# Up projection of a squared-ReLU MLP: one 512-column matmul against both parts of the activations, in place of two of 256

## The chip, the cores and the metric

The kernel runs on one core of one Trainium2 chip. The metric is device time in microseconds, the median of several runs. The engines are named as the profile names them: PE is TensorE's matmul, PEld its weight load, DVE is VectorE, ACT is ScalarE, POOL is GpSimd, SP is SyncE, which here issues nearly all transfers.

## The reference

One decoder layer on 256 positions of 2048 features, all in fp32: RMSNorm, an input projection to two groups of eight heads (forgetting attention, dilated attention), group norms, an output projection, then the MLP with squared ReLU, and a final norm. The change concerns the first product of the MLP:

```
h = rms_norm(x, norm2_g[l])
x = x + jnp.square(jax.nn.relu(h @ w_mlp_in[l])) @ w_mlp_out[l]
return rms_norm(x, final_norm_g)
```

`w_mlp_in` is 2048 x 8192, `w_mlp_out` 8192 x 2048.

## The kernel before

**Precision by parts.** Each fp32 operand is split in two parts of the type float32r: `hi`, a rounded copy, and `lo`, the remainder. A product of two operands is the sum of three matmuls into the same PSUM columns: hi x hi, hi x lo and lo x hi. Activations stand in SBUF by feature: `aT_hi` and `aT_lo` hold 16 tiles (kt) of 128 features x 256 positions each, `hT_hi` and `hT_lo` (which are the buffers `big_hi` and `big_lo`) the same for the hidden layer.

**Chunks and steps.** All weights are streamed once, in chunks of 512 columns: 12 chunks for q, v and k, 8 for the output projection, then four rounds of 4 chunks "u" (up) and 4 chunks "d" (down). A round covers 2048 of the 8192 hidden features. An up or down chunk has 16 kt, two to a step, so 8 steps. For a step the weights of two kt arrive in `raw` (four buffers, two steps each, DMA issued by SP), ACT rounds them into `whi` (line 178) and DVE takes the remainder into `wlo` (line 179); both pools hold four steps.

**Two ways of multiplying.** For "q", "k" and "u" (`TURNED`) the weights are the stationary operand, in blocks of 128 columns, and the activations stream, 256 columns at a time (`turned_product`, line 340): per kt 4 blocks x 3 matmuls. Two blocks share a PSUM bank of 512 columns. The result is already by feature. For "o", "v" and "d" the activations are stationary and 512 weight columns stream (`product`, lines 323 to 325): per kt 2 halves of the positions x 3 matmuls.

**The drain of an up chunk** (`drain_u`) takes each of the two banks through relu (ACT, 626), a square (DVE, 627), the rounded part (ACT, 261) and the remainder (DVE, 262) into `hT_hi` and `hT_lo`.

**What sets the order.** The order is written out by hand; each engine runs its own instructions in that order. Ahead of step i's matmuls stands the split of step i + 3 (`LEAD`), and small work is hung behind single kt by `at(...)`: the drain of a chunk behind its last kt. So on ACT and DVE the drain stands behind the split for three steps ahead and before the split for the step after that. The last chunk of all has a loop of its own (`last_chunk`), and the weights of its first four steps are split into the place of `aT_hi` and `aT_lo`, which nobody needs any more. The PSUM pool has four banks named "acc", two named "sc" and two named "tr", eight in all; "sc" and "tr" serve the attention and the transposes before the MLP.

Of the kernel before, what the change touches and what calls it, by code (L numbers as in the profile page):

```python
# [11 lines left out]
F32 = mybir.dt.float32  # L12
F32R = mybir.dt.float32r
BF16 = mybir.dt.bfloat16
AF = mybir.ActivationFunctionType
ALU = mybir.AluOpType
# [3 lines left out]
P = 128  # L20
D_MODEL = 2048
SEQ = 256
# [5 lines left out]
KT = D_MODEL // P  # L28
CW = 512
# [44 lines left out]
def kernel(  # L74
# [18 lines left out]
    nc = tc.nc  # L93
# [7 lines left out]
    two = ctx.enter_context(tc.tile_pool(name="two", bufs=2))  # L101
    wraw = ctx.enter_context(tc.tile_pool(name="wraw", bufs=4))
    wsplit = ctx.enter_context(tc.tile_pool(name="wsplit", bufs=LEAD + 1))
    wide = ctx.enter_context(tc.tile_pool(name="wide", bufs=1))
    few = ctx.enter_context(tc.tile_pool(name="few", bufs=1))
    psum = ctx.enter_context(tc.tile_pool(name="psum", bufs=2, space=PSUM))
# [4 lines left out]
    chunks = []  # L111
# [25 lines left out]
    raws, splits = {}, {}  # L137
# [15 lines left out]
    def split(i, j0=0, n=2):  # L153
        if i >= len(steps):
            return
        if j0:
            return split_rows(i, j0, n)
        ci, s = steps[i]
        if ci == len(chunks) - 1 and s < 4:
            hi, lo = (a[:, 4 * s:4 * s + 4, :].rearrange("p (k j) s -> p k (j s)", k=2) for a in (aT_hi, aT_lo))  # L160
        else:
            what, cols = chunks[ci][0], chunks[ci][5]
            high, low = (HIGH, LOW) if what in TURNED else (NEAR, NEAR) if cols == CW else (GATED, HIGH - NEAR)
            hi, lo = (
                wsplit.tile([P, 2 * CW + LINE], F32R, name=n)[:, b:b + 2 * cols].rearrange("p (j c) -> p j c", j=2)
                for n, b in (("whi", high), ("wlo", low))
            )
        splits[i] = (hi, lo)
        split_rows(i, j0, n)

    def split_rows(i, j, n):
        ci, s = steps[i]
        hi, lo = (a[:, j:j + n, :] for a in splits[i])
        t = raws[ci, s // 2][:, 2 * (s % 2) + j:2 * (s % 2) + j + n, :chunks[ci][5]]
        cols = t.shape[2]
        step = cols // 2 if i == j == 0 else cols
        for c in range(0, cols, step):
            nc.scalar.activation(hi[:, :, c:c + step], t[:, :, c:c + step], AF.Copy)  # L178
        nc.vector.tensor_tensor(lo, t, hi.bitcast(F32), op=ALU.subtract)  # L179
# [68 lines left out]
        nc.vector.tensor_copy(gT[:, k0:k1], p[:, k0:k1])  # L248

    wide.tile([P, NEAR], F32, name="ahead")  # L250
    aT_hi = wide.tile([P, KT, SEQ], F32R, name="aT_hi")
    aT_lo = wide.tile([P, KT, SEQ], F32R, name="aT_lo")

    def split_psum(hi, lo, src, scale=None, early=False):

        if early:

            nc.vector.tensor_scalar(hi, src, scale, None, op0=ALU.mult)
            nc.vector.scalar_tensor_tensor(lo, src, scale, hi.bitcast(F32), op0=ALU.mult, op1=ALU.subtract)
        elif scale is None:  # L260
            nc.scalar.activation(hi, src, AF.Copy)  # L261
            nc.vector.tensor_tensor(lo, src, hi.bitcast(F32), op=ALU.subtract)  # L262
        else:
            nc.scalar.activation(hi, src, AF.Copy, scale=scale)
            nc.vector.scalar_tensor_tensor(
                lo, src, scale, hi.bitcast(F32), op0=ALU.mult, op1=ALU.subtract
            )
# [42 lines left out]
    accs = {}  # L310

    def operands(what, key):
        if what == "o":
            return yT_hi, yT_lo, key[0] * NH
        if what == "d":
            return hT_hi, hT_lo, 0
        return aT_hi, aT_lo, 0

    def product(acc, a, kt, t, w, j, cols, go, end):

        (ah, al, base), (hi, lo) = a, w
        xh, xl = (p[:, base + kt, t * P:(t + 1) * P] for p in (ah, al))
        nc.tensor.matmul(acc, xh, hi[:, j, cols], start=go, stop=False, skip_group_check=True)  # L323
        nc.tensor.matmul(acc, xl, hi[:, j, cols], start=False, stop=False, skip_group_check=True)  # L324
        nc.tensor.matmul(acc, xh, lo[:, j, cols], start=False, stop=end, skip_group_check=True)  # L325

    def turned_product(ci, i, j, kt, kts):


        if kt == 0:  # L330
            accs[ci] = [psum.tile([P, CW], F32, name="acc", bufs=4) for _ in range(2)]
        hi, lo = splits[i]
        terms = ((hi, aT_hi), (hi, aT_lo), (lo, aT_hi))
        order = [(b, n) for b in range(4) for n in range(3)]
        if i == j == 0:
            order.sort(key=lambda bn: bn[1])
        for b, n in order:
            acc = accs[ci][b // 2][:, b % 2 * SEQ:(b % 2 + 1) * SEQ]
            w, a = terms[n]
            nc.tensor.matmul(acc, w[:, j, b * P:(b + 1) * P], a[:, kt, :],  # L340
                             start=kt == 0 and b % 2 == 0 and n == 0, stop=kt == kts - 1 and n == 2,
                             skip_group_check=True)

    def products(i, j):
        ci, s = steps[i]
        what, key, _, _, _, cols, kts = chunks[ci]
        kt = 2 * s + j
        if what in TURNED:
            return turned_product(ci, i, j, kt, kts)
        a = operands(what, key)  # L350
        if cols > CW:
            return gated_products(ci, i, j, kt, kts, a)
        if kt == 0:
            accs[ci] = [psum.tile([P, CW], F32, name="acc", bufs=4) for _ in range(TB)]
        go, end = kt == 0, kt == kts - 1
        for t in range(TB):
            product(accs[ci][t], a, kt, t, splits[i], j, slice(0, CW), go, end)

    def gated_products(ci, i, j, kt, kts, a):

        if kt == 0:
            accs[ci] = [psum.tile([P, 512], F32, name=n, bufs=k) for n, k in (("acc", 4), ("acc", 4), ("sc", 2))]
        half = CW // 2
        for t in range(TB):
            for acc, c0, c1, go in ((accs[ci][0][:, t * half:(t + 1) * half], 0, half, t == 0),
                                    (accs[ci][1 + t][:, :half + NH], half, CW + NH, True)):
                product(acc, a, kt, t, splits[i], j, slice(c0, c1), go and kt == 0, kt == kts - 1)
# [252 lines left out]
    def drain_u(c, ci):  # L620


        acc = accs.pop(ci)
        for half in range(2):
            h = two.tile([P, CW], F32, name="nat")
            nc.scalar.activation(h, acc[half], AF.Relu)
            nc.vector.tensor_tensor(h, h, h, op=ALU.mult)
            k0 = 4 * c + 2 * half
            split_psum(
                hT_hi[:, k0:k0 + 2, :].rearrange("p k s -> p (k s)"),  # L630
                hT_lo[:, k0:k0 + 2, :].rearrange("p k s -> p (k s)"), h,
            )
# [82 lines left out]
    for ci, (what, key, *_rest) in enumerate(chunks[:-1]):  # L715
# [9 lines left out]
        elif what in "qk":  # L725
            for half in range(2):
                late = half if what == "k" else (2 if key else 8) + 5 * half
                at(e + late, drain_qk, key, what, ci, half)
            if what == "k":
                kind = groups[key][4]  # L730
                for h in range(4):
                    n = e + 6 + 7 * (h // 2)
                    if kind == 0:
                        at(n - 3, decay_of, groups[key][3] * 4 + h)
                    at(n, scores, key, h)
                for h in range(4):
                    at(e + 20 + 7 * (h // 2), values, key, h)
                for h in range(4):
                    at(e + 13 + 7 * (h // 2), turn_probs, key, h)
                if key % 2:  # L740
                    at(e + 33, group_norm, kind)
        elif what == "o":
            at(e, drain_o, *key, ci)
            if key[0] == 1:
                for n in range(2):
                    at(e + 2, to_features, 4 * key[1] + 2 * n, 16)
                if key[1] == 3:
                    at(e + 4, second_norm)
        elif what == "u":
            at(e, drain_u, key[1], ci)  # L750
        else:
            at(e, drain_d, *key, ci)
            if key == (ROUNDS - 1, 0):
                at(e - 8, load_gf)

    idle_products(WARM)
    for k in range(2):
        to_features(k, 0, 1)
        split(0, k, 1)
    idle_products(WARM2)  # L760
    at(0, gains, 2, 16)
    at(0, to_features, 2, 0, 1)
    at(0, split, 1, 0, 1)
    at(0, to_features, 3, 0, 1)
    at(0, split, 1, 1, 1)
# [58 lines left out]
```

## Time and profile before

| | |
|---|---|
| median of 3 runs | 1104.33 us (1104.29 to 1105.59) |
| span of the profiled execution | 1214.1 us |
| its own time beside the span | none is given; the span is the first to the last instruction |
| granted TensorE clock, mean over the span | 0.850 |
| TensorE matmuls | 7373, in progress 1201.8 us |
| TensorE weight loads | 7373, in progress 1070.3 us |
| VectorE, ScalarE | 655.5 and 521.1 us busy |
| DMA | 209.17 MB, mean 172 GB/s |

The page and the views beside it are of one profiled execution, which is longer than the runs. A row of a group gives the source line, the engine, the operation, the tiles written and read, the shapes and the count, then busy time in us and the mean of one in ns, then the engine's idle time before it and who ended it. A row of the timeline gives the start and the length in us. Matmuls overlap, so that the length of one is more than the distance from one to the next; the distances are what counts.

### The profile page before, as it was taken

What the parts mean: (1) busy time and instruction counts of PE and PEld (TensorE: products, weight loads), DVE (VectorE), ACT (ScalarE), POOL (GpSimd) and SP (SyncE); (2) the same over time, 40 slices, a digit from 0 to 9 for tenths busy, and PEclk for the clock granted to TensorE, in tenths of its full rate; (3) what the DMA queues carried; (4) which work ended last, traced back from release to release, by engine and by line L of the source; (5) the groups of instructions that cost most, each with busy time, mean ns of one, the idle gap of its engine ahead of it and who ended that gap; (6) DMA issues with size and microseconds to landing.
All of it is one profiled execution on the core that took longest, in us unless ns stands there. A gap on an engine that the chain in (4) does not pass through costs nothing.

```text
span 1214.1 us, 17573 instructions
## 1 busy us (share of the span) xinstructions
PE 1201.8 (99%) x7373; PEld 1070.3 (88%) x7373; DVE 655.5 (54%) x837; ACT 521.1 (43%) x687; POOL 27.3 (2%) x42
## 2 busy tenths in 40 slices
PE   9999999999999999999999999999999999999997
PEld 8999898998987799987789997779998779998776
DVE  5666656556566655544544455445545444555563
ACT  5454535445444544443334443334444333444341
POOL 0010200000000000000000000000000000000000
PEclk8888888888888888888888888888888888888887
DMA  8664553544544455555555545555655555545541
GB/s 300 200 209 139 169 178 112 190 160 139 184 153 165 148 174 173 161 187 175 176 175 175 173 170 187 179 170 158 194 183 178 174 173 173 174 147 222 187 139 70
DMA packets 105387, 209.17 MB, mean 172 GB/s; under 512 B 3971, under 2 KB 5084, under 8 KB 105180
## 3 DMA queue, kind: packets, MB, share of 16 engines
q1 hardware_dynamic: 104412, 206.59, 51.6%
q8 instruction: 57, 0.93, 0.3%
q0 software_dynamic: 304, 1.06, 0.2%
q10 hardware_dynamic: 592, 0.40, 0.1%
q14 instruction: 22, 0.18, 0.0%
HBM read 205.93 MB, written 2.11 MB: 171 GB/s over the span
## 4 chain that ended last, share of the span: by engine, by line
PE 99%; DMA 0%; DVE 0%; issue 0%; ACT 0%; POOL 0%; ACTq 0%; DVEq 0%
PE acc L340 48%; PE acc L324 16%; PE acc L323 16%; PE acc L325 16%; PE tr L275 1%; PE sc L575 1%; PE sc L531 0%; PE tr L559 0%; DMA xs<-in_x_dram 0%; PE sc L527 0%; PE sc L577 0%; PE sc L323 0%; PE sc L324 0%; PE sc L325 0%; PE sc L521 0%
## 5 line engine op out<-in xcount | busy, mean ns | idle before, releaser
L179 DVE TENSOR_TENSOR wlo<-raw,whi 128x1024 fp32r<-128x1024 f32 (+2 forms) x382 | 464.0, 1223 | 416.9 <-ACT whi L178 414.8
L178 ACT ACTIVATE whi<-raw 128x1024 fp32r<-128x1024 f32 (+2 forms) x383 | 398.7, 1051 | 475.0 <-PE acc L340 230.1
L340 PE MATMUL acc<-aT_hi,whi 128*128 128x256 f32 x1536 | 450.5, 294 | 0.0
L340 PE MATMUL acc<-aT_hi,wlo 128*128 128x256 f32 x1536 | 446.3, 291 | 0.0
L340 PE MATMUL acc<-aT_lo,whi 128*128 128x256 f32 x1536 | 445.7, 291 | 0.0
L340 PEld LDWEIGHTS acc<-aT_hi,whi 128*128 128x128 f32 x1536 | 306.0, 199 | 1.5 <-ACT p L261 0.7
L340 PEld LDWEIGHTS acc<-aT_lo,whi 128*128 128x128 f32 x1536 | 304.8, 199 | 0.4
L340 PEld LDWEIGHTS acc<-aT_hi,wlo 128*128 128x128 f32 x1536 | 304.9, 199 | 0.0
L324 PE MATMUL acc<-whi,big_lo 128*128 128x512 f32 (+1 forms) x632 | 262.4, 415 | 0.0
L323 PE MATMUL acc<-whi,big_hi 128*128 128x512 f32 (+1 forms) x632 | 262.2, 415 | 0.0
L325 PE MATMUL acc<-wlo,big_hi 128*128 128x512 f32 (+1 forms) x632 | 260.6, 412 | 0.0
L323 PEld LDWEIGHTS acc<-whi,big_hi 128*128 128x128 f32 x632 | 121.6, 192 | 36.1
L325 PEld LDWEIGHTS acc<-wlo,big_hi 128*128 128x128 f32 x632 | 121.6, 192 | 35.9
L324 PEld LDWEIGHTS acc<-whi,big_lo 128*128 128x128 f32 x632 | 121.7, 193 | 34.6
L323 PE MATMUL acc<-whi,aT_hi 128*128 128x512 f32 (+1 forms) x144 | 54.7, 380 | 0.0
L324 PE MATMUL acc<-whi,aT_lo 128*128 128x512 f32 (+1 forms) x144 | 54.1, 376 | 0.0
L325 PE MATMUL acc<-wlo,aT_hi 128*128 128x512 f32 (+1 forms) x144 | 54.1, 376 | 0.0
L262 DVE TENSOR_TENSOR big_lo<-nat,big_hi 128x512 fp32r<-128x512 f32 x32 | 22.2, 692 | 22.4 <-ACT big_hi L261 22.4
L650 DVE SCALAR_TENSOR_TENSOR xs<-acc,rstd2sq,xs 128x512 f32<-128x512 f32 (+1 forms) x33 | 24.2, 734 | 16.2 <-PE acc L325 16.2
L325 PEld LDWEIGHTS acc<-wlo,aT_hi 128*128 128x128 f32 x144 | 27.7, 192 | 5.5
L323 PEld LDWEIGHTS acc<-whi,aT_hi 128*128 128x128 f32 x144 | 27.9, 194 | 5.2
L324 PEld LDWEIGHTS acc<-whi,aT_lo 128*128 128x128 f32 x144 | 27.9, 194 | 5.1
(167 smaller groups left out, 508.4 us busy)
## 6 DMA issues: line engine op xcount, KB each, us to landing
raw<-in_w_mlp_in_dram SPq DMA_DIRECT2D x64, 1024.0 KB, 5.3
raw<-in_w_mlp_out_dram SPq DMA_DIRECT2D x64, 1024.0 KB, 5.1
raw<-in_w_in_dram SPq DMA_DIRECT2D x42, 1024.0 KB, 5.0
raw<-in_w_out_dram SPq DMA_DIRECT2D x16, 1024.0 KB, 5.1
raw<-in_w_in_dram SPq DMA_DIRECT2D x4, 1040.0 KB, 8.1
xs<-in_x_dram SPq DMA_DIRECT2D x3, 512.0 KB, 9.8
raw<-in_w_in_dram SPq DMA_DIRECT2D x2, 512.0 KB, 5.7
big_lo<-rel_d POOLq DMA_DIRECT2D x1, 1024.0 KB, 7.0
```

The source lines that it names most:

```text
L178: nc.scalar.activation(hi[:, :, c:c + step], t[:, :, c:c + step], AF.Copy)
L179: nc.vector.tensor_tensor(lo, t, hi.bitcast(F32), op=ALU.subtract)
L262: nc.vector.tensor_tensor(lo, src, hi.bitcast(F32), op=ALU.subtract)
L275: nc.tensor.transpose(p[:, j * SEQ + t * P:j * SEQ + (t + 1) * P], xs[:, t, c:c + P], ident)
L323: nc.tensor.matmul(acc, xh, hi[:, j, cols], start=go, stop=False, skip_group_check=True)
L324: nc.tensor.matmul(acc, xl, hi[:, j, cols], start=False, stop=False, skip_group_check=True)
L325: nc.tensor.matmul(acc, xh, lo[:, j, cols], start=False, stop=end, skip_group_check=True)
L340: nc.tensor.matmul(acc, w[:, j, b * P:(b + 1) * P], a[:, kt, :], start=kt == 0 and b % 2 == 0 and n == 0, stop=kt == kts - 1 and n == 2, s ...
L575: nc.tensor.matmul(y[:, :SEQ], v[:, 0, dims], p[:, m, :SEQ], start=n == 0, stop=False, skip_group_check=True)
L650: nc.vector.scalar_tensor_tensor(xs[:, t, cs], acc[:, :cs.stop - cs.start], rstd2sq[:, t:t + 1], xs[:, t, cs], op0=ALU.mult, op1=ALU.add)
```

## The change

For the up projection alone, `aT_hi` and `aT_lo` become the two halves of one tile `aT`, kt by kt, so that hi and lo of one kt lie side by side as 512 columns. A new function, `paired_product`, gives each block of 128 weight columns a PSUM bank of its own. Per block and kt the hi weights are loaded once, and all 512 columns stream past them: the left half of the bank collects hi x hi, the right half hi x lo. Then the lo weights are loaded and the 256 columns of hi stream into the right half. At the chunk's end the two halves are added, and relu and square become one operation. A chunk takes four banks: two "acc", and two "sc" or two "tr" in turn. "q" and "k" are multiplied as before, with `aT_hi` and `aT_lo` as views.

```diff
         if ci == len(chunks) - 1 and s < 4:
-            hi, lo = (a[:, 4 * s:4 * s + 4, :].rearrange("p (k j) s -> p k (j s)", k=2) for a in (aT_hi, aT_lo))
+            hi, lo = (aT[:, 4 * s + 2 * n:4 * s + 2 * n + 2].rearrange("p k j s -> p k (j s)") for n in range(2))
...
-    aT_hi = wide.tile([P, KT, SEQ], F32R, name="aT_hi")
-    aT_lo = wide.tile([P, KT, SEQ], F32R, name="aT_lo")
+    aT = wide.tile([P, KT, 2, SEQ], F32R, name="aT")
+    aT_hi, aT_lo = aT[:, :, 0], aT[:, :, 1]
...
+    def paired_product(ci, i, j, kt, kts):
+        if kt == 0:
+            rest = ("sc", "tr")[chunks[ci][1][1] % 2]
+            accs[ci] = [psum.tile([P, CW], F32, name=n, bufs=k) for n, k in (("acc", 4), ("acc", 4), (rest, 2), (rest, 2))]
+        hi, lo = splits[i]
+        for b, acc in enumerate(accs[ci]):
+            w = slice(b * P, (b + 1) * P)
+            nc.tensor.matmul(acc.rearrange("p (n s) -> p n s", n=2), hi[:, j, w], aT[:, kt],
+                             start=kt == 0, stop=False, skip_group_check=True)
+            nc.tensor.matmul(acc[:, SEQ:], lo[:, j, w], aT[:, kt, 0],
+                             start=False, stop=kt == kts - 1, skip_group_check=True)
...
+        if what == "u":
+            return paired_product(ci, i, j, kt, kts)
         if what in TURNED:
             return turned_product(ci, i, j, kt, kts)
...
         for half in range(2):
             h = two.tile([P, CW], F32, name="nat")
-            nc.scalar.activation(h, acc[half], AF.Relu)
-            nc.vector.tensor_tensor(h, h, h, op=ALU.mult)
+            n = two.tile([P, CW], F32, name="nat")
+            for k in range(2):
+                part, bank = n[:, k * SEQ:(k + 1) * SEQ], acc[2 * half + k]
+                nc.scalar.activation(part, bank[:, SEQ:], AF.Copy)
+                nc.vector.tensor_tensor(part, bank[:, :SEQ], part, op=ALU.add)
+            nc.vector.scalar_tensor_tensor(h, n, 0.0, n, op0=ALU.max, op1=ALU.mult)
             k0 = 4 * c + 2 * half
```

How the instructions stand, at three places. First TensorE at the first kt of the first up chunk, before; a row is a matmul with its weight load, the numbers tell buffers apart, and `acc_4256` and `acc_4257` are the two banks:

```order
L340 MATMUL acc_4256<-aT_hi_127,whi_4194 128x256
L340 MATMUL acc_4256<-aT_lo_128,whi_4194 128x256
L340 MATMUL acc_4256<-aT_hi_127,wlo_4195 128x256
L340 MATMUL acc_4256<-aT_hi_127,whi_4194 128x256
L340 MATMUL acc_4256<-aT_lo_128,whi_4194 128x256
L340 MATMUL acc_4256<-aT_hi_127,wlo_4195 128x256
L340 MATMUL acc_4257<-aT_hi_127,whi_4194 128x256
L340 MATMUL acc_4257<-aT_lo_128,whi_4194 128x256
L340 MATMUL acc_4257<-aT_hi_127,wlo_4195 128x256
```

The same place now, the whole kt, with four banks:

```order
L353 MATMUL acc_4255<-aT_127,whi_4193 128x512
L355 MATMUL acc_4255<-aT_127,wlo_4194 128x256
L353 MATMUL acc_4256<-aT_127,whi_4193 128x512
L355 MATMUL acc_4256<-aT_127,wlo_4194 128x256
L353 MATMUL sc_4257<-aT_127,whi_4193 128x512
L355 MATMUL sc_4257<-aT_127,wlo_4194 128x256
L353 MATMUL sc_4258<-aT_127,whi_4193 128x512
L355 MATMUL sc_4258<-aT_127,wlo_4194 128x256
```

Three rows of 256 to a block have become one of 512 and one of 256. Next VectorE at the end of that chunk, before, from the drain to the next splits:

```order
L627 TENSOR_TENSOR nat_4512<-nat_4512 128x512
L262 TENSOR_TENSOR big_lo_142<-nat_4512,big_hi_141 128x512
L627 TENSOR_TENSOR nat_4517<-nat_4517 128x512
L262 TENSOR_TENSOR big_lo_142<-nat_4517,big_hi_141 128x512
L179 TENSOR_TENSOR wlo_4523<-raw_4342,whi_4522 128x1024
```

And now:

```order
L646 TENSOR_TENSOR nat_4450<-acc_4255,nat_4450 128x256
L646 TENSOR_TENSOR nat_4450<-acc_4256,nat_4450 128x256
L647 SCALAR_TENSOR_TENSOR nat_4449<-nat_4450 128x512
L262 TENSOR_TENSOR big_lo_141<-nat_4449,big_hi_140 128x512
L646 TENSOR_TENSOR nat_4459<-sc_4257,nat_4459 128x256
L646 TENSOR_TENSOR nat_4459<-sc_4258,nat_4459 128x256
L647 SCALAR_TENSOR_TENSOR nat_4458<-nat_4459 128x512
L262 TENSOR_TENSOR big_lo_141<-nat_4458,big_hi_140 128x512
L179 TENSOR_TENSOR wlo_4468<-raw_4327,whi_4467 128x1024
```

Four adds of half a bank have come in ahead of the next split, which stands where it stood. Last ScalarE at the same place, before:

```order
L626 ACTIVATE nat<-acc 128x512
L261 ACTIVATE big_hi<-nat 128x512
L626 ACTIVATE nat<-acc 128x512
L261 ACTIVATE big_hi<-nat 128x512
L178 ACTIVATE whi<-raw 128x1024 x8
```

And now:

```order
L645 ACTIVATE nat<-acc 128x256 x2
L261 ACTIVATE big_hi<-nat 128x512
L645 ACTIVATE nat<-sc 128x256 x2
L261 ACTIVATE big_hi<-nat 128x512
L178 ACTIVATE whi<-raw 128x1024 x8
```

A relu of 512 columns has become two copies of 256; the splits of the next chunk's eight steps follow as before.

## The prediction, made before the changed kernel ran

> **What bounds the kernel now.** I read the page first, then the chain of work that ended last in order of time, then the busy time of two neighbouring stretches.
>
> ```profile
> span 1214.1 us, 17573 instructions
> PE 1201.8 (99%) x7373; PEld 1070.3 (88%) x7373; DVE 655.5 (54%) x837; ACT 521.1 (43%) x687; POOL 27.3 (2%) x42
> PE 99%; DMA 0%; DVE 0%; issue 0%; ACT 0%; POOL 0%; ACTq 0%; DVEq 0%
> ```
>
> The chain is TensorE from end to end: it hardly waits for anyone. The question is what TensorE itself is held by: the columns that stream through the array, or the weight loads, which it starts as often as matmuls (7373 each).
>
> ```profile
> 627.47 96.33 PE acc L340 x768
> 820.13 96.33 PE acc L340 x768
> ```
>
> These rows of the chain are two whole up-projection stages (round 1 and round 2): 4 chunks x 16 kt x 12 matmuls = 768 each, none missing. Between them, from 627.47 + 96.33 = 723.80 to 820.13, lies the down projection of round 1. The two stretches side by side (the count takes in a neighbour's at the edge):
>
> ```profile
> core 0: us, PE busy (x) PEld busy (x) DVE busy (x) ACT busy (x) POOL busy (x), PEclk, DMA share, GB/s
> 627.47:723.80 96.33, 96.33 (x769) 96.33 (x769) 47.85 (x47) 40.72 (x45) 0.00 (x0) 0.85 0.55 176
> 723.80:820.13 96.33, 96.33 (x386) 73.82 (x386) 46.93 (x43) 35.67 (x36) 0.00 (x0) 0.85 0.53 173
> ```
>
> This is the central reading. The up projection does 768 matmuls of 256 columns, the down projection 384 of 512: both 196,608 columns. The first has twice the matmuls and twice the weight loads, and its loads are in progress 96.33 of 96.33 us, against 73.82. Yet both take 96.33 us. A matmul of 256 costs 96.33/768 = 0.1254 us, one of 512 costs 96.33/384 = 0.2509. So time goes by columns, at one granted clock (0.85), and the 384 additional loads and matmuls cost nothing to within the 0.01 us of the rows. A load row that is always busy is no proof that loads bind.
>
> **How this execution stands to the runs.** The median of the three runs is 1104.33 us, 109.8 below the profiled span; nothing on the page tells of time around the span, so I take the span as the execution's own time.
>
> ```profile
> 0.00:8.00 8.00, 5.64 (x16) 1.00 0.70 194
> 8.00:10.00 2.00, 2.00 (x12) 0.96 1.05 387
> 10.00:1200.00 1190.00, 1188.73 (x7307) 0.85 0.52 173
> 1205.46:1214.10 8.64, 0.00 (x0) 0.58 0.32 122
> ```
>
> (TensorE alone: length, busy, granted clock, DMA.) The clock falls from 1.00 to 0.85 around 9 us and stays there; after 1205.46 no matmul runs. If the runs differ from the profile by their clock alone, the 1195.5 us from 10 to 1205.46 take 1104.33 - 18.6 = 1085.7 in them: an estimated mean clock of 0.85 x 1195.5/1085.7 = 0.936. Nothing shows that clock directly, and this is the weak point of the forecast.
>
> **The change part by part.** *Matmuls and loads.* Per block of 128 weights and kt, three matmuls of 256 with three loads become one of 512 and one of 256 with two loads. Sixteen chunks x 16 kt x 4 blocks = 1024 such groups: 1024 loads and 1024 matmuls vanish (of 7373), the columns stay at 1024 x 768. By the stretches above: before 3 x 0.1254 = 0.376 us, after 0.2509 + 0.1254 = 0.376. Worth 0 in this execution. The cover that makes it so is the stream itself: each load lies under the matmul before it.
>
> How close are loads to binding? In the head work, 128-column transposes stand back to back, with half the columns of an up-projection matmul to hide a load (first row: loads; the others: transposes):
>
> ```profile
> 112.00 0.73 PEld L559 LDWEIGHTS tr<-ident,pr 128*128 128x128 f32 x6
> 12.57 0.42 PE L275 MATMUL tr<-ident,xs 128*128 128x128 f32 x2
> 6.17 0.90 PE L275 MATMUL tr<-ident,xs 128*128 128x128 f32 x3 [1.18 <-DMA xs<-in_x_dram]
> 4.57 0.42 PE L275 MATMUL tr<-ident,xs 128*128 128x128 f32 x1
> L559 PEld LDWEIGHTS tr<-ident,pr 128*128 128x128 f32 x48 | 5.6, 144 | 0.0
> L275 PE MATMUL tr<-ident,xs 128*128 128x128 f32 x64 | 11.7, 302 | 1.2 <-DMA xs<-in_x_dram 1.2
> ```
>
> With 0.14 us for a single such load (144 ns), six in 0.73 are (0.73 - 0.14)/5 = 0.118 us apart. A load thus paces at some 0.118 us where 0.1254 is to be covered: hidden, but by 6% only. After the change two loads (0.236) stand under 0.376.
>
> The Trainium skill, "TensorE: Matmul & The Clock Gate", section "LDWEIGHTS (loading the stationary operand)", puts a load at columns / 1.2 ns, an estimate of 106.7 ns for 128; the trace's 118 decides here. By the page's figure loads would stay hidden at a clock of 0.936 too, where a matmul of 256 takes 0.1254 x 0.85/0.936 = 0.114 us, and the sum would be the same 0.
>
> *The layout* (aT in one tile, kt by kt) changes addresses, no instruction: 0. The rows that split a weight for the last chunk into aT's place are the same in number.
>
> *The drain* of a chunk grows, on ACT and DVE. Round 1's first chunk ends at 627.47 + 24.08 = 651.55:
>
> ```profile
> 650.83 0.60 ACT L626 ACTIVATE nat<-acc 128x512 f32<-128x512 f32 x1 [1.32 <-PE acc L340]
> 652.19 0.63 ACT L261 ACTIVATE big_hi<-nat 128x512 fp32r<-128x512 f32 x1 [0.76 <-DVE nat L627]
> 652.73 0.58 ACT L626 ACTIVATE nat<-acc 128x512 f32<-128x512 f32 x1
> 654.18 0.63 ACT L261 ACTIVATE big_hi<-nat 128x512 fp32r<-128x512 f32 x1 [0.88 <-DVE nat L627]
> 654.72 2.00 ACT L178 ACTIVATE whi<-raw 128x1024 fp32r<-128x1024 f32 x2
> 651.46 0.69 DVE L627 TENSOR_TENSOR nat<-nat 128x512 f32<-128x512 f32 x1 [0.69 <-ACT nat L626]
> 652.85 0.69 DVE L262 TENSOR_TENSOR big_lo<-nat,big_hi 128x512 fp32r<-128x512 f32 x1 [0.70 <-ACT big_hi L261]
> 655.79 2.36 DVE L179 TENSOR_TENSOR wlo<-raw,whi 128x1024 fp32r<-128x1024 f32 x2 [0.26 <-ACT whi L178]
> ```
>
> Queued behind the drain on both engines is the split of the weights of step i+4 (i the chunk's last step). It starts at 654.72 and its wlo is done at 655.79 + 1.23 = 657.02. TensorE wants it three steps after the chunk's end: 651.55 + 3 x 24 x 0.1254 = 660.58. The slack is 3.56 us.
>
> The new operations by their nearest rows: the copy of half a bank like L584, the add like L663 (from SBUF) or the 256-column L650 (from PSUM), the max-and-multiply like L627 above (0.69).
>
> ```profile
> L584 ACT ACTIVATE sqt<-sc 128x256 f32<-128x256 f32 x14 | 5.4, 384 | 5.6 <-DVE sc L583 5.6
> L650 DVE SCALAR_TENSOR_TENSOR xs<-acc,rstd2sq,xs 128x256 f32<-128x256 f32 x2 | 1.0, 484 | 5.5 <-PE acc L325 5.5
> L663 DVE TENSOR_TENSOR xs<-xs,relT 128x256 f32<-128x256 f32 x2 | 0.8, 420 | 0.6 <-ACT nat L657 0.6
> L650 DVE SCALAR_TENSOR_TENSOR xs<-acc,rstd2sq,xs 128x512 f32<-128x512 f32 x31 | 23.2, 750 | 10.7 <-PE acc L325 10.6
> ```
>
> I take 0.38 for a copy and 0.45 for an add, between the two rows. Per chunk ACT goes from 2 x 0.60 + 2 x 0.63 = 2.46 to 4 x 0.38 + 1.26 = 2.8, DVE from 4 x 0.69 = 2.8 to 4 x 0.45 + 2.8 = 4.6: 4 chunks add 7 us to DVE's 47.85 of 96.33. In time: the first copy can begin one block earlier (650.45), the second at 650.83; add to 651.7, max-and-multiply to 652.4, big_hi to 653.0, big_lo to 653.7 with both copies of the second half beside it; two adds to 654.5, max-and-multiply to 655.2, big_hi to 655.8. The split then starts near 655.7 instead of 654.72, 1.0 us late, and the slack is still 2.6. At the runs' 0.936 three steps are 8.2 us and it is 1.8. Worth 0; what hides it is LEAD = 3.
>
> Who else waits for the drain: the down projection wants the last chunk's hT only at kt 12, three quarters into its first chunk (18 us). The four banks of a chunk (two of "acc", two of "sc" or "tr") are written again two chunks, 48 us, later. DMA queues: SP issues the same transfers in the same order; a raw buffer is freed up to 1 us later, with four in turn of 6 us each.
>
> **Sum:** 1214.1 + 0 + 0 = 1214.1 profiled, 1104.3 for the runs.
>
> **The rivals.** *1. Loads bind in the runs, though not in the profile.* If a load keeps its 0.118 us while a matmul of 256 shrinks with the clock, the runs' q, k and u matmuls (4608) are paced by loads. Then 4608 x 0.118 = 544 of the 1085.7 us, the other 1195.5 - 4608 x 0.1254 = 617.7 take 542, the clock is 0.85 x 617.7/542 = 0.969, and the change takes the up projection from 3072 x 0.118 = 362.5 to 1024 x 0.376 x 0.85/0.969 = 337.8: 25 less, 1080. For: the 6% margin. Against: loads follow the clock, since transposes before the array was in its stride are (0.90 - 0.42)/2 = 0.24 apart (row at 6.17, one alone 0.42) and later 0.42 - 0.30 = 0.12 (row at 12.57, one alone 0.302).
>
> *2. The clock answers to the load.* It dropped once the matmuls stood close together; with a third fewer loads in a third of the time a higher one may be granted. Against: it is 0.85 in both stretches above, one with half the loads. The up projection takes some 4 x 96.33 x 0.85/0.936 = 350 us of a run; from 0 to full clock there, 350 x 0.064 = 22 less: 1082 to 1104.
>
> *3. A fixed cost per matmul.* If all that lies between the runs and full clock, 1085.7 - 1195.5 x 0.85 = 69.5 us, were a cost per matmul, 69.5/7373 = 9.4 ns, the 1024 that vanish give 9.7: 1095; against it stand the equal 96.33 us. The Trainium skill, same page, section "Wait — 56ns, not 53.3ns?", has about 2.5 ns on each matmul at the full array clock and none at the half clock; by it the sum would be 2.6 us less, an estimate. At 0.85 the trace shows none.
>
> *4. Slower: the drain makes the split late.* It decides once the drain grows by over 3.56 us in the profile, 8.2 - (657.02 - 651.55) = 2.7 in the runs. If half-bank operations cost as whole ones (0.60, 0.75 by L650's 512 form) and none overlapped, the growth is 2 x 0.60 + 4 x 0.75 = 4.2: 1.5 late at 16 chunks, 24 more: 1128. Half of that already needs every bound to fail.
>
> That fewer loads are not what comes out is no rival: the instructions in order show two matmuls a block.
>
> **How the numbers follow.** A measurement tells 0.2% (2.2 us) from no change. No change 0.52; rival 1 0.17, since the clock of the runs isn't seen; rival 2 0.13; rival 3 0.06, half of it under 2.2 us; rival 4 0.06; slower otherwise (a lower clock, a bank or port disputed) 0.06. Faster 0.17 + 0.13 + 0.03 = 0.33, same 0.55, slower 0.12. The forecast's own range is 1102 to 1106.5. The range reaches to 1080, taking in rivals 2 and 3 and the near end of 1, and to 1107; beyond lie the far part of rival 1 and the slower cases, under 0.2.
>
> **What would show it.** In the profile after: up-projection stretches of 96.33 us with 512 matmuls each, 6349 in all; loads there no longer busy throughout; the first split after a drain some 1 us later, with no TensorE idle time behind it; clock 0.85 and span 1214. Wrong would be: an unchanged span but shorter runs (rival 1 or 3), a clock above 0.85 (rival 2), TensorE waiting for whi or wlo at a chunk's fourth step (rival 4).

## The result and the profile after

The change makes the kernel slower: 1119.05 us (median of 4, 1118.68 to 1119.28) against 1104.31 us (4 runs, 1103.56 to 1105.59). The ratio is 1.0132, with a 95% interval of 1.0118 to 1.0146: 13.0 to 16.1 us. The profiled execution took 1119.28 us, of which 1117.5 are its span.

To read its profile one number has to be set right first. The profile of before had a granted clock of 0.85; this one has 1.00, and so has every execution since, those of the kernel before included (0.995 to 0.998 as means). So the kernel before was profiled again (e1 below). Here are the pages of the two at the same clock, first the changed kernel, then the kernel before:

```profile
span 1117.5 us, 15621 instructions
PE 1103.8 (99%) x6349; PEld 968.9 (87%) x6349; DVE 673.6 (60%) x901; ACT 521.8 (47%) x719; POOL 27.9 (2%) x42
PEclk9999999999999999999999999999999999999998
PE 98%; DMA 0%; DVE 0%; issue 0%; ACT 0%; POOL 0%; ACTq 0%; DVEq 0%
```

```profile
span 1101.6 us, 17573 instructions
PE 1089.4 (99%) x7373; PEld 999.7 (91%) x7373; DVE 649.2 (59%) x837; ACT 521.0 (47%) x687; POOL 27.9 (3%) x42
PEclk9999999999999999999999999999999999999999
```

The chain is still TensorE throughout, 1024 matmuls and loads are gone as they should be, and the span is 15.9 us longer. The place is seen by stages. Round 1's up projection and the down projection behind it, first of the changed kernel, then of the kernel before (length, busy time of PE, PEld, DVE, ACT, POOL, then the clock):

```profile
575.26:665.68 90.42, 90.42 (x514) 79.08 (x513) 52.65 (x60) 41.15 (x52) 0.00 (x0) 1.00 0.59 187
665.68:752.75 87.07, 87.07 (x386) 72.08 (x385) 47.40 (x46) 35.61 (x37) 0.00 (x0) 1.00 0.59 192
```

```profile
569.88:656.94 87.06, 87.06 (x770) 87.06 (x769) 47.58 (x46) 40.88 (x45) 0.00 (x0) 1.00 0.61 195
656.94:744.00 87.06, 87.06 (x386) 72.07 (x385) 46.39 (x43) 35.64 (x37) 0.00 (x0) 1.00 0.59 192
```

The down projection is the same to 0.01 us. The up projection takes 90.42 us instead of 87.06, with TensorE busy throughout: it does not wait, its matmuls stand further apart. Four rounds of 3.36 us are 13.4 of the 14.7. (The two profiled spans differ by 15.9 because this execution of the changed kernel also lost 2.0 us at its start: the 221 matmuls that the kernel before has begun by 31 us it has begun by 33, with a granted clock of 0.95 in that stretch.) The timeline shows the step, start and length of each row, first the changed kernel, then the kernel before:

```profile
580.04 0.40 PE L353 MATMUL sc<-aT,whi 128*128 128x512 f32 x1
580.27 0.28 PE L355 MATMUL sc<-aT,wlo 128*128 128x256 f32 x1
580.39 0.40 PE L353 MATMUL sc<-aT,whi 128*128 128x512 f32 x1
580.62 0.28 PE L355 MATMUL sc<-aT,wlo 128*128 128x256 f32 x1
580.74 0.40 PE L353 MATMUL acc<-aT,whi 128*128 128x512 f32 x1
```

```profile
580.00 0.28 PE L340 MATMUL acc<-aT_hi,whi 128*128 128x256 f32 x1
580.12 0.28 PE L340 MATMUL acc<-aT_lo,whi 128*128 128x256 f32 x1
580.23 0.28 PE L340 MATMUL acc<-aT_hi,wlo 128*128 128x256 f32 x1
580.34 0.28 PE L340 MATMUL acc<-aT_hi,whi 128*128 128x256 f32 x1
```

From block to block it is 0.35 now and was 0.34. Taken over the stages' regular parts the distances are 233.3 + 120.0 = 353.3 ns against 3 x 113.3 = 340.0. The difference of 13.3 ns for 1024 blocks is 13.7 us, which lies in the interval of the result.

Two theories followed. Theory A: the pace of TensorE at this clock is not set by columns alone, and this sequence of matmuls and loads gets a worse one; in form A1 because of where weights and stream lie in SBUF relative to each other, in form A2 because widths of 512 and 256 alternate. Theory B: the drain, the four banks or the layout make TensorE late.

### The profile page after: what moved, and what is told of

It reads as the page before. It is cut to its first block, busy times and chain, and to the rows that moved or that the text cites. A ratio compares the mean times of both kernels' runs of the same rounds, so it can differ in the third digit from the quotient of the medians.

```text
span 1117.5 us, 15621 instructions
## 1 busy us (share of the span) xinstructions
PE 1103.8 (99%) x6349; PEld 968.9 (87%) x6349; DVE 673.6 (60%) x901; ACT 521.8 (47%) x719; POOL 27.9 (2%) x42
## 4 chain that ended last, share of the span: by engine, by line
PE 98%; DMA 0%; DVE 0%; issue 0%; ACT 0%; POOL 0%; ACTq 0%; DVEq 0%
PE acc L340 16%; PE acc L323 16%; PE acc L325 15%; PE acc L324 15%; PE acc L353 11%; PE acc L355 5%; PE tr L353 5%; PE sc L353 5%; PE tr L355 3%; PE sc L355 3%; PE tr L275 1%; PE sc L591 1%; PE sc L547 1%; DMA xs<-in_x_dram 0%; PE tr L575 0%; PE sc L543 0%
## 5 line engine op out<-in xcount | busy, mean ns | idle before, releaser
L353 PE MATMUL acc<-aT,whi 128*128 128x512 f32 x512 | 192.1, 397 | 0.0
L340 PE MATMUL acc<-aT,whi 128*128 128x256 f32 x1024 | 178.2, 279 | 0.0
L340 PEld LDWEIGHTS acc<-aT,whi 128*128 128x128 f32 x1024 | 155.0, 189 | 1.1 <-issue 0.9
L355 PE MATMUL acc<-aT,wlo 128*128 128x256 f32 x512 | 144.8, 283 | 0.0
L340 PE MATMUL acc<-aT,wlo 128*128 128x256 f32 x512 | 141.5, 278 | 0.0
L353 PEld LDWEIGHTS acc<-aT,whi 128*128 128x128 f32 x512 | 96.7, 189 | 22.6
L355 PEld LDWEIGHTS acc<-aT,wlo 128*128 128x128 f32 x512 | 96.8, 189 | 0.1
L340 PEld LDWEIGHTS acc<-aT,wlo 128*128 128x128 f32 x512 | 96.4, 189 | 0.0
L353 PE MATMUL tr<-aT,whi 128*128 128x512 f32 x256 | 96.0, 397 | 0.0
L353 PE MATMUL sc<-aT,whi 128*128 128x512 f32 x256 | 96.0, 397 | 0.0
L355 PE MATMUL tr<-aT,wlo 128*128 128x256 f32 x256 | 72.5, 283 | 0.0
L355 PE MATMUL sc<-aT,wlo 128*128 128x256 f32 x256 | 72.4, 283 | 0.0
L353 PEld LDWEIGHTS tr<-aT,whi 128*128 128x128 f32 x256 | 48.4, 189 | 11.3
```

The lines of the kernel that those rows point to most:

```text
L353: nc.tensor.matmul(acc.rearrange("p (n s) -> p n s", n=2), hi[:, j, w], aT[:, kt], start=kt == 0, stop=False, skip_group_check=True)
L355: nc.tensor.matmul(acc[:, SEQ:], lo[:, j, w], aT[:, kt, 0], start=False, stop=kt == kts - 1, skip_group_check=True)
```

## The experiments

**e1, the kernel before again.** No edit.

> The kernel before, unchanged, looked at again for its own profile at the clock that the changed kernel's profile had (1.00 granted). Theory A (the pace of a matmul beside its load is not set by columns alone, and the pair of 512 and 256 is paced worse than three of 256): matmuls of the up projection 113 to 114 ns apart as those of q and k are in the changed kernel's profile (113), 3 x 113.3 = 340 ns a block against the 353 of the changed kernel; an up-projection stage of 87.0 us against 90.4; span 1102 to 1104. Theory B (the drain or the banks make TensorE wait): the same 113 ns, but a stage of 87 us must then come from fewer gaps, and the changed kernel's 353 would not fill its 90.4 us. If the clock is 0.85 again: 125.4 ns, and this run says nothing.

1103.37 us, span 1101.6, clock 0.998; its rows stand above. Its 256-column matmuls are 113.3 ns apart, its 512-column ones 226.7. Theory A's numbers came out. At this clock, too, up and down projection take the same time with 768 and 384 loads.

**e2, three matmuls of 256 in the changed kernel's frame.**

```diff
-            nc.tensor.matmul(acc.rearrange("p (n s) -> p n s", n=2), hi[:, j, w], aT[:, kt],
-                             start=kt == 0, stop=False, skip_group_check=True)
+            for n in range(2):
+                nc.tensor.matmul(acc[:, n * SEQ:(n + 1) * SEQ], hi[:, j, w], aT[:, kt, n],
+                                 start=kt == n == 0, stop=False, skip_group_check=True)
```

> The changed kernel with its four banks, its layout and its drain, but with each 512 parted in two of 256 with the same weights: the matmuls and loads of before. Theory A: the time of before, 1104 (within 3 us), 113 ns from matmul to matmul, an up-projection stage of 87.0 us. Theory B (drain, banks or layout): it stays with the changed kernel, 1117 to 1120.

1105.39 us (10 runs) against 1105.32 (13 runs): ratio 1.0005, interval 0.9995 to 1.0015. The same stage:

```profile
571.25:658.31 87.06, 87.06 (x769) 87.02 (x769) 52.28 (x60) 41.36 (x52) 0.00 (x0) 1.00 0.60 194
```

Drain, banks and layout are those of the changed kernel (DVE is busy for 52.28 us, as there for 52.65), the matmuls those of before, and so is the time. Theory B falls: all of the loss lies in the pair of matmuls.

**e3, sixteen pairs of offsets in one run.** Each up chunk starts its split weights elsewhere.

```diff
+            if what == "u":
+                r, c = chunks[ci][1]
+                high, low = 8 + 8 * r, 8 + 8 * c
```

> The changed kernel with another pair of starting offsets in SBUF for each of the 16 up chunks: whi at 8, 16, 24, 32 columns in rounds 0 to 3, wlo at 8, 16, 24, 32 in chunks 0 to 3 (the changed kernel has 24 and 56, the streaming aT begins at 8). Theory A1 (the pace depends on where weights and streaming operand lie relative to each other): a block takes between 327 and 360 ns depending on the pair, in steps of some 6.7 ns; at equal offsets (8 and 8) the 512 takes 226.7 as in the down projection, and some pair brings the block to 340 or under. Theory A2 (it is the change of width from 512 to 256 and back): 353 ns for all 16 pairs, and a time like that of the changed kernel, 1119.

1113.36 us. A chunk has 64 blocks, so 353.3 ns a block are 22.61 us and 340 are 21.76. The four chunks of round 2 (whi at 24; wlo at 8, 16, 24, 32), TensorE alone:

```profile
749.42:771.19 21.77, 21.77 (x130) 1.00 0.61 193
771.19:793.38 22.19, 22.19 (x130) 1.00 0.60 191
793.38:815.99 22.61, 22.61 (x130) 1.00 0.59 190
815.99:838.60 22.61, 22.61 (x130) 1.00 0.54 187
```

Same instructions, same widths, another offset: a chunk goes from 22.61 to 21.77 us. That speaks for theory A1, and A2 cannot be the whole cause. Of the sixteen pairs only 24 with 8 gives 340 ns, the others 347 to 353 (of the first chunk, which has transposes in it, only the regular part counts). None lies below 340. One part of A1 did not come: at 8 and 8 a 512 was expected to take 226.7, as in the down projection, and takes 231.5. And each pair was entered only once here. e10 will show that how a chunk is entered can matter too, so that the scan alone does not settle the value of a single pair; e5 and e12 settle it for 24 with 8 and 24 with 56.

**e4, the four matmuls of 512 first, then the four of 256.**

```diff
         for b, acc in enumerate(accs[ci]):
             w = slice(b * P, (b + 1) * P)
             nc.tensor.matmul(acc.rearrange("p (n s) -> p n s", n=2), hi[:, j, w], aT[:, kt],
                              start=kt == 0, stop=False, skip_group_check=True)
+        for b, acc in enumerate(accs[ci]):
+            w = slice(b * P, (b + 1) * P)
             nc.tensor.matmul(acc[:, SEQ:], lo[:, j, w], aT[:, kt, 0],
```

> The changed kernel with the matmuls of a kt in another order: the four of 512 first, then the four of 256. Theory A2 (the change of width costs): six of eight transitions are between equal widths, so the block falls from 353 to some 343 and the run to about 1109. Theory A1 (offsets): the same widths with the same offsets, 353 and 1119, or any change only through which weight loads under which stream: loads of whi now lie under 512 and loads of wlo mostly under 256. Theory B: 1119.

1112.34 us, ratio 1.0065 (1.0050 to 1.0080). Round 1's up projection, TensorE alone:

```profile
572.75:661.94 89.19, 89.19 (x513) 1.00 0.58 192
```

That is 348 ns a block, neither 353 nor 343: most changes of width are gone, and 8 of the 13 ns a block are still there. This run does not tell A1 from A2; it says that at the same offsets the order matters too.

**e5, the best pair of the scan.**

```diff
+            if what == "u":
+                high, low = HIGH, NEAR
```

> The changed kernel with wlo of the up chunks at 8 instead of 56, whi at 24 as it was. Nothing else differs. Theory A1 (offsets of weights against the stream): 227 + 113 = 340 ns a block as in the one chunk of the scan that had this pair, an up-projection stage of 87.0 us, and the time of before within 0.2% (1103 to 1107). A theory in which the widths as such cost: 353 ns and 1119.

1107.51 us (11 runs) against 1104.11 (15 runs): ratio 1.0023, interval 1.0014 to 1.0032. Of the 14.7 us this one number brings back about 11, but not all: the time lies just beyond the 1103 to 1107 that were expected. A chunk of round 0 and one of round 1:

```profile
440.55:462.95 22.40, 22.40 (x130) 1.00 0.58 191
615.98:637.74 21.76, 21.76 (x130) 1.00 0.60 195
```

Rounds 1 to 3 run at 340 ns a block, round 0 at 350, steady through all its chunks, with the same instructions at the same offsets. 256 blocks x 10 ns are 2.6 us, within the interval of what remains (1.5 to 3.5 us). e10 takes this up.

**e6, the kernel before with weights and stream at equal offsets.**

```diff
+            if what == "u":
+                high, low = NEAR, NEAR
```

> The kernel before with whi and wlo of the up chunks at 8, where the streaming aT begins too (it has 24 and 56). Theory A1: a matmul of 256 goes from 113.3 to about 120 ns (as the last chunk's 256-wide ones in the changed kernel's profile, which lie at equal offsets), 3072 x 6.7 = 20 us, time 1125. If offsets matter only where widths change: 113.3 and the time of before, 1105.

1125.02 us, ratio 1.0188 (1.0172 to 1.0203), 20.9 us more, forecast 20.

```profile
575.45:667.60 92.15, 92.15 (x770) 92.15 (x769) 47.83 (x47) 40.73 (x45) 0.00 (x0) 1.00 0.57 185
667.60:754.67 87.07, 87.07 (x387) 72.08 (x386) 46.42 (x43) 35.66 (x36) 0.00 (x0) 1.00 0.59 191
```

92.15/768 = 120.0 ns a matmul, where 24 and 56 have 113.3. No width changes anywhere in this kernel's up projection, so offsets cost by themselves. The kernel before relies on its pair of offsets; the change kept the pair and altered what it was paired with.

**e7, widths apart, at four offsets.** Chunks 0 and 2 of a round do the 512s alone, chunks 1 and 3 three 256s.

```diff
+            if what == "u":
+                high = low = 8 + 8 * chunks[ci][1][0]
...
+            if chunks[ci][1][1] % 2 == 0:
...
+                continue
+            for n, weights in ((0, hi), (1, hi), (1, lo)):
+                nc.tensor.matmul(acc[:, n * SEQ:(n + 1) * SEQ], weights[:, j, w], aT[:, kt, 0], ...)
```

> Widths kept apart: in up chunks 0 and 2 of each round only the matmuls of 512 are done (hi weights; the product of the lo weights is left out), in chunks 1 and 3 three matmuls of 256 per block, all on the hi part of the activations (the hi weights times the lo part is left out). Weights at 8, 16, 24, 32 in rounds 0 to 3, the stream at 8. Theory A1 with the rule that a load goes by the matmul it lies under: 512 takes 227 at offset 8 and 233 at 24; 256 takes 120 at 8 and 113 at 24; 16 and 32 lie between. If the width change is what costs: 227 and 113 at all offsets.

A chunk of 512s and one of 256s at offset 8, then the same at 24:

```profile
435.10:449.80 14.70, 14.70 (x66) 1.00 0.55 180
449.80:472.85 23.05, 23.05 (x194) 1.00 0.73 252
759.82:774.77 14.95, 14.95 (x66) 1.00 0.55 176
774.77:797.39 22.62, 22.62 (x194) 1.00 0.75 259
```

The regular distances: 512s 227 ns at 8 and 233 at 24, as expected, again without a change of width. 256s 120 at 8, but 118 at 24, where 113 was expected. At 16 and 32, expected between, the 512s take 233 and 234 and the 256s 117 to 119. So my rule, that each load goes by its offset and by the matmul over it, is too simple: whi at 24 with wlo at 24 is not whi at 24 with wlo at 56.

**e8, finer offsets.**

```diff
+                high, low = (20, 24, 28, 56)[r], (4, 8, 12, 40)[c]
```

> The scan with other offsets: whi at 20, 24, 28, 56 in rounds 0 to 3, wlo at 4, 8, 12, 40 in chunks 0 to 3. Theory A1 with a period of 32 columns: 24 and 56 give the same for whi, 8 and 40 the same for wlo (340 ns a block for those four pairs), 20 and 28 and 4 and 12 lie a few ns above. If some pair goes under 340, the paired form could be faster than before; at 325 (the columns of a block at 2.4 per ns are 320) it would win 15 us.

1112.14 us. 24 with 8, 24 with 12, 24 with 40, then 56 with 40:

```profile
595.71:617.47 21.76, 21.76 (x130) 1.00 0.61 194
617.47:639.23 21.76, 21.76 (x130) 1.00 0.60 197
639.23:661.63 22.40, 22.40 (x130) 1.00 0.56 192
992.02:1014.21 22.19, 22.19 (x130) 1.00 0.55 187
```

The period of 32 columns did not show: 24 with 40 takes 350 where 24 with 8 takes 340, and no pair with 56 comes to 340. It is not refuted either, since each pair was entered once and 350 is also what 24 with 8 takes in round 0 of e5. With whi at 24, wlo at 4, 8 or 12 gives 340. Again nothing lies under 340: of the 31 different pairs in the two scans the best is as fast as three matmuls of 256.

**e9, shorter loads, and the offsets of the down projection.** The lo products of the up projection are left out; beyond the first kt its 512s load 128, 64, 64, 32 weight columns in rounds 0 to 3.

```diff
+            elif what == "d":
+                high = low = 4 * (4 * r + c)
...
+            m = P if kt == 0 else (128, 64, 64, 32)[chunks[ci][1][0]]
+            nc.tensor.matmul(acc[:m]..., hi[:, j, b * P:b * P + m], aT[:, kt], ...)
```

> What sets the 226.7 ns of a matmul of 512 (213.3 at 2.4 columns per ns)? The lo products of the up projection are left out, and beyond the first kt its matmuls of 512 use fewer weight columns: all 128 in round 0, 64 in rounds 1 and 2, 32 in round 3 (weights at 8, 8, 24, 8; outputs beyond are left out). Besides, the 16 down chunks have their streaming weights at offsets 0, 4, 8, ... 60, whole and unchanged otherwise. If reading the weights collides with the stream: 226.7 in round 0, about 220 with 64 weight columns, 216 to 218 with 32. If the stream has this pace of its own (0.443 ns per column): 226.7 in all four. In the down projection: 226.7 at offset 8 and up to 237 elsewhere if the offsets against each other decide; an offset under 226.7 would be a gain to take.

Shorter loads gain nothing: medians of 227 ns with 128 weight columns, 230 with 64 (232 in the round at offset 24), 232 with 32 (these chunks at times wait for weights, so only matmuls that follow without a wait are counted). The length of a load is thus not what keeps a 512 from the 2 x 125.4 x 0.85 = 213 ns that the clock alone would give. In the down projection, chunks at offsets 4, 8, 12 and 24:

```profile
483.08:505.48 22.40, 22.40 (x97) 1.00 0.55 187
505.48:527.26 21.78, 21.78 (x97) 1.00 0.57 188
527.26:549.50 22.24, 22.24 (x97) 1.00 0.60 192
656.34:678.32 21.98, 21.98 (x97) 1.00 0.58 188
```

Of the fifteen whole chunks the one at 8, which both kernels use, is the shortest (96 x 226.7 ns); the rest take 21.98 to 22.49.

**e10, the start of a stage moved in time.** e5 with one short matmul ahead of up chunks 1, 2 and 3 of each round.

```diff
+        r, c = chunks[ci][1]
+        if kt == 0 and c:
+            n = (64, 128, 192)[c - 1] + 16 * r
+            nc.tensor.matmul(accs[ci][0][:, :n], hi[:, 0, :P], aT[:, 0, 0, :n], start=True, stop=True, ...)
```

> The changed kernel with whi at 24 and wlo at 8, which ran at 340 ns a block in rounds 1 to 3 and at 350 in round 0. At the start of chunks 1, 2 and 3 of each round one additional matmul of 64, 128, 192 columns (and 16 more per round) goes into the bank before it is started; its result is overwritten. If the pace also depends on how the stage falls in step in time: some chunk of round 0 changes to 340, or some of the rounds 1 to 3 change to 350. If round 0 is slower for another reason (what the other engines do, the data): round 0 stays at 350 and the others at 340.

1113.75 us. Chunks 0 and 1 of round 1, then chunks 1, 2 and 3 of round 3:

```profile
575.03:596.84 21.81, 21.81 (x130) 1.00 0.61 191
596.85:619.39 22.54, 22.54 (x130) 1.00 0.59 190
949.59:971.49 21.90, 21.90 (x130) 1.00 0.60 192
971.49:994.04 22.55, 22.55 (x131) 1.00 0.58 195
994.04:1015.81 21.77, 21.77 (x130) 1.00 0.55 188
```

One additional matmul sends round 1 from 340 to 350 ns a block, and it stays there (round 2 does the same); in round 3 a second one sends it to 350 and a third one back to 340. So at offsets 24 and 8 there are two steady paces, and what runs just ahead of a chunk decides between them. Whether it does so by the moment at which the stream enters or in another way is not shown. Round 0 stayed at 350 behind all three of its own, so that moving it to 340 was not shown.

**e11 and e12, the same additional matmuls in the kernel before and in the changed kernel.** The edit is that of e10, without the offsets; in e11 into the first of the two banks, with `aT_hi` as the stream.

> The kernel before with the same additional matmuls as in the run before this one, at the start of up chunks 1 to 3 of each round. If its form (three of 256, offsets 24 and 56) falls back into one step whatever the moment: 113.3 ns in all 16 chunks. If it too has a second step: 117 to 120 ns in some chunks behind an additional matmul.

1107.57 us. Chunk 1 of round 1 with its additional matmul:

```profile
594.07:615.96 21.89, 21.89 (x196) 1.00 0.62 192
```

That is the additional matmul and 64 blocks of 340 ns (21.76 us), and it is 340 in every chunk. The form before falls back into its pace at once.

> The changed kernel as it was (offsets 24 and 56) with the additional matmuls. If offsets alone set its pace: 353 ns a block in all 16 chunks. If 24 and 56 also have two steps and it was merely always in the worse one: some chunks at 340.

1118.57 us. Three of its chunks:

```profile
596.32:619.04 22.72, 22.72 (x132) 1.00 0.59 185
619.04:641.76 22.72, 22.72 (x131) 1.00 0.57 189
951.86:974.58 22.72, 22.72 (x132) 1.00 0.58 186
```

353.3 ns a block in the steady part of all 16. With these entries the changed kernel as written has one pace, the worse one.

No run points to a version that beats both: three matmuls and the pair share a best of 340 ns a block, which is 0.443 ns a column, and the down projection's 226.7 are the same 0.443.

What stays open is why. The runs show that the offsets of the weights, the order of the widths and, at 24 and 8, what runs ahead of a chunk decide between steady paces; they do not show what it is that collides. The stream of the up projection began at 8 in every run, so whether the offsets count against the stream's, against each other or by themselves is not shown. Writes of ACT and DVE into the split weights are not what decides: in round 1 of the changed kernel's profile 18 blocks pass while neither of them works, and they take 353 ns like the rest.

## Why the prediction was wrong

**The step that failed** is the term "Matmuls and loads", put at 0. The price after the change, 0.2509 + 0.1254 us a block, was added up from two stages that each run one width: 512 in the down projection, 256 in the up projection, each with its own operands in their own places. The sum takes it that a matmul keeps its price beside one of another width and with its weights elsewhere. It does not: in the runs the block takes 233.3 + 120.0 = 353.3 ns where the same sum gives 226.7 + 113.3 = 340.0, and 1024 blocks of 13.3 ns are 13.7 of the 14.7 us. The clock is not what misled here. At the runs' clock e1 has equal stages again (87.06 and 87.06 us), and the same reasoning would have given the same 0. The layout was put at 0 because it "changes addresses, no instruction". e2 bears out that 0, but not its reason: in e6 addresses alone cost 6.7 ns a matmul. Whether the pair is free at a clock of 0.85 was not tried, since the clock is not ours to set.

**The estimated clock of 0.936** was wrong too. I took the whole 109.8 us between profile and runs for the clock. In truth the clock is 0.998, and a column takes 0.443 ns instead of the 125.4 x 0.85/256 = 0.416 that the clock alone would give: 6% that I read as throttling. That there had to be a second limit in the runs was the rivals' business, and the prediction priced it as loads that bind (rival 1) or as a cost per matmul (rival 3), from both of which fewer loads could only gain. The limit was of a third kind, for which a pair of matmuls is not the same as three. A cost per matmul does not show: in e1 512 columns take twice the time of 256. Rival 3's rule from the Trainium skill ("TensorE: Matmul & The Clock Gate", section "Wait — 56ns, not 53.3ns?": columns / 2.4 ns and about 2.5 ns a matmul at the full clock) gives an estimate of 215.8 and 109.2 ns; the trace has 226.7 and 113.3 and does not agree.

**The forecast that loads do not bind** was right, for the profile and for the runs: after the change PEld is busy 79.08 of 90.42 us where it was busy throughout, and no time is gained. e9 adds that even a load of a quarter of the columns gains nothing. The same page of the Trainium skill, section "Step-by-step: what each phase is for", says that loading the next weights takes no read bandwidth from the running matmul. e6 is at odds with that as far as addresses go: moving nothing but the weights, by 16 and 48 columns, changes 113.3 ns to 120.0.

**The drain** went as forecast. The groups and the timeline after round 1's first chunk, which ends at 575.26 + 22.61 = 597.87:

```profile
L645 ACT ACTIVATE nat<-acc 128x256 f32<-128x256 f32 x32 | 11.8, 384 | 13.2 <-PE acc L355 13.2
L646 DVE TENSOR_TENSOR nat<-acc,nat 128x256 f32<-128x256 f32 x32 | 12.4, 425 | 0.0
602.12 1.05 ACT L178 ACTIVATE whi<-raw 128x1024 fp32r<-128x1024 f32 x1
603.20 2.36 DVE L179 TENSOR_TENSOR wlo<-raw,whi 128x1024 fp32r<-128x1024 f32 x2 [0.26 <-ACT whi L178]
```

A copy took 0.384 us (forecast 0.38), an add 0.425 (0.45). The split starts 4.25 us behind the chunk's end, where it was 3.17: 1.1 late, forecast 1.0. Its wlo is done at 604.43, wanted at 597.87 + 3 x 22.61/8 = 606.35: slack 1.9, forecast 1.8. e2 shows that this costs nothing in the runs: rival 4 did not happen.

**Rival 2**, a higher clock for fewer loads: the clock is 0.995 to 0.998 with either number of loads. The chance of a slower time was put at 0.12, half of it for "slower otherwise (a lower clock, a bank or port disputed)", which comes nearest to what happened but had no price; the range ended at 1107.

## What to carry to other kernels

Prices read in two stages that each run one width need not add up for a stage that mixes them or has its operands at other offsets: time such a mixture before an edit of TensorE's stream is priced at nothing. When the span of a profile and the time of the runs differ by 10%, get a profile at the runs' clock too: the distances changed here from 125.4 to 113.3 ns, less than the clock did. Loads that are already hidden were worth nothing when they went, and the width and order of matmuls was not free to choose: offsets in SBUF that suit one form (24 and 56 here) can be the wrong ones for the next. They can be swept sixteen at a time in a single launch, one pair for each chunk, and a pair that looks good must also hold however the stage is entered.

## What was not expected of the hardware

At a granted clock of 1.00 a float32r column takes 0.443 ns at best, at 0.85 it takes 0.490: the clock rises by 18%, the pace by 11%. A chunk keeps one steady pace from block to block, but which one depends on more than its columns: 113.3 to 120.0 ns for 256 columns among their like, 226.7 to 234.3 for 512, and 340.0 to 360.0 for a block of 768. The offsets of the weights decide it, the order and, at one pair of offsets, what runs just ahead of the chunk.
